# A two-layer decoder trunk in FP32: the offset term of two blocks of the last layer norm made on TensorE

## The chip, the cores and the metric

The kernel runs on one core of a Trainium2 chip. A core has five engines with queues of their own: PE (TensorE: matrix products into PSUM, with the weight loads shown apart as PEld), DVE (VectorE), ACT (ScalarE), POOL (GpSimd) and SP (SyncE, which here issues DMAs). The metric is the time of one execution on the device in microseconds (us), as a median of several runs.

## The reference, cut to what matters

Two layers over 256 positions of width 2048. The first has a gated short convolution, the second latent attention; each is followed by an MLP of width 8192 with squared ReLU, and each sub-layer ends in a layer norm of the scaled input plus the sub-layer's output. What matters here is the very last line, the layer norm behind the second MLP.

```python
def layer_norm(x, g, b):
    mu = jnp.mean(x, axis=-1, keepdims=True)
    var = jnp.mean(jnp.square(x - mu), axis=-1, keepdims=True)
    return (x - mu) * lax.rsqrt(var + LN_EPS) * g + b
...
for layer in range(2):
    mix = short_conv_mixer(...) if layer == 0 else mla_mixer(...)
    h = layer_norm(ALPHA * h + mix, ln_g[layer, 0], ln_b[layer, 0])
    h = layer_norm(ALPHA * h + sq_relu_mlp(h, ...), ln_g[layer, 1], ln_b[layer, 1])
return h
```

## The kernel before, in words

All products are made from FP32 values split into a high and a low part in a reduced format (`hi`, `lo`, type fp32r), with two or three TensorE products for each. Weights come from memory in pieces of 128 x 1024 into a pool of six buffers (`raws`, tag "raw"); ACT writes the high part, DVE subtracts it and writes the low part, into a ring of eight (`whl`). Activations stay in SBUF for the whole run. PSUM has eight banks of 128 x 512, in two pools of four, and `psum(name)` (line 228) takes one.

The order on each engine is made by a scheduler at build time. It goes through the instructions in the order in which the program wrote them, as a priority, and puts an instruction earlier where its engine would have nothing else that is ready. Only where `state["kept"]` is a set does the wrapper `Engine` (lines 60 to 79) pin it: the first instruction of each engine after that point is left free, and each further one goes behind the one written before it on its engine. So it is in the long middle of an MLP, whose order a planner (`Work`, lines 582 to 715) writes out. Everything around the change below is left to the scheduler.

**The start.** Lines 347 to 354 set a 128 x 128 tile `ones` (and two columns of `col`) and run ten TensorE products of `ones` with itself into a bank that nobody reads, while the first input is on its way (lines 527 to 542: sixteen rows of input and weights, converted by ACT and DVE as they land, then multiplied).

**The means' column.** `Norm.means` (line 387) makes one small column, `off`, in a buffer of its own, once, at the end of the first MLP's planned part.

**The end.** `to_out` (line 1331) takes over when the planned part of the second MLP is done. The result is held as 4 column blocks of 512 (n = 0 to 3) for 2 groups of 128 positions (t = 0, 1), each `block(n, t)` of 128 x 512 in SBUF. `turn_residual` adds the transposed input. The norm's gain and offset, `gbt`, spread over all 128 partitions, are loaded: `gbt[:, n, :BW]` is g of block n, `gbt[:, n, BW:]` is b. Then `down` (line 306) makes the last part of the products `ps_d` for blocks 0 and 1, both t together, and `down_late` (line 318) for blocks 2 and 3: first both blocks of t = 0, then both of t = 1. After each product `put` adds it into the block (DVE), and `counted` takes the block's statistics (DVE). When block 3 of a t is done, `finished` (line 1341) joins the statistics to mean and variance (`mv`), makes r = 1/sqrt(var + eps) in `rsqrt` (line 361: one ACT square root and four small DVE operations, `iv`, `rt`, `ra`, `rr`), and for each of the four blocks does two DVE operations and one DMA to the output:

```python
u = (d - mean) * g          # scalar_tensor_tensor, 128 x 512
d = u * r + b               # scalar_tensor_tensor, 128 x 512
sync.dma_start(out[...], d)
```

(The first two lines are lines 1354 and 1355 in short form.) The output of t = 0 is made while TensorE still works on t = 1; that of t = 1 comes after all products.

Of the kernel before, what the change touches and what calls it, by code (L numbers as in the profile page):

```python
# [10 lines left out]
F32 = mybir.dt.float32  # L11
F32R = mybir.dt.float32r
AF = mybir.ActivationFunctionType
ALU = mybir.AluOpType
AX = mybir.AxisListType

P = 128
# [16 lines left out]
NB = 4  # L34
BW = D // NB
# [18 lines left out]
def trunk(ctx: ExitStack, tc: tile.TileContext, opening, xT, vecs, w_in, w_out, w_kv, w_q, w_uk, w_uv,  # L54
          w_qn, w_qp, w_o, w1, w2, w2f, cosT, sinT, mask, ident, gb, out):
    nc = tc.nc
    PS = bass.MemoryType.PSUM
    state = {"made": 0, "next": 2 * OPEN, "kept": None}
# [22 lines left out]
    scalar, vector, tensor, sync = (Engine(e) for e in (nc.scalar, nc.vector, nc.tensor, nc.sync))  # L81
    const = ctx.enter_context(tc.tile_pool(name="const", bufs=1))
    act = ctx.enter_context(tc.tile_pool(name="act", bufs=1))
    raws = ctx.enter_context(tc.tile_pool(name="raws", bufs=RAW))
    whl = ctx.enter_context(tc.tile_pool(name="whl", bufs=WA))
    tmp = ctx.enter_context(tc.tile_pool(name="tmp", bufs=2))
    small = ctx.enter_context(tc.tile_pool(name="small", bufs=2))
# [5 lines left out]
    def array(tag, dtype, name, *dims):  # L93

        n = int(np.prod(dims))
        t = act.tile([P, ROOM[tag] // 4], dtype, tag=tag, name=name)[:, :n]
        names = "uvwxyz"[:len(dims)]
        return t.rearrange(f"p ({' '.join(names)}) -> p {' '.join(names)}", **dict(zip(names, dims)))
# [38 lines left out]
    start = [0]  # L137
# [3 lines left out]
    class Banks:  # L141
# [15 lines left out]
        @classmethod  # L157
        def next(cls):
            cls.count += 1
            if cls.only is not None:  # L160
                return cls.only
            return cls.more if cls.more is not None and cls.count % 8 >= 4 else pmm
# [65 lines left out]
    def psum(name):  # L228
        return Banks.next().tile([P, 512], F32, tag="mm", name=name)
# [76 lines left out]
    def down(x, put, n):  # L306

        ps = [psum("ps_d") for _ in range(2)]
        for j in range(len(x) // 2):
            w, = take(1)  # L310
            for kk in range(2):
                k = 2 * j + kk
                for t in range(2):
                    dot(ps[t], wide_rows(w, kk), held(x[k], t), k == 0, k == len(x) - 1)
        for t in range(2):
            put(n, t, ps[t])

    def down_late(x, put, blocks):

        ws = {}  # L320
        for t in range(2):
            for n in blocks:
                ps = psum("ps_d")
                for k in range(len(x)):
                    if (n, k // 2) not in ws:
                        ws[n, k // 2], = take(1)
                    dot(ps, wide_rows(ws[n, k // 2], k % 2), held(x[k], t), k == 0, k == len(x) - 1)
                put(n, t, ps)
# [17 lines left out]
    id_t = const.tile([P, P], F32, name="id_t")  # L346
    ones = const.tile([P, P], F32, name="ones")
    col = const.tile([P, COL], F32, name="col")
    vector.memset(ones, 1.0 / P)
    warm = psum("warm")  # L350
    for _ in range(WARM):
        tensor.matmul(warm[:, :P], ones, ones, start=True, stop=True)
# [5 lines left out]
        sync.dma_start(cos_t, cosT)  # L358
        sync.dma_start(sin_t, sinT)

    def rsqrt(out, ve):

        n = ve.shape[-1]
        s, iv, t, a = (small.tile([P, 2], F32, tag=g, name=g)[:, :n] for g in ("sq", "iv", "rt", "ra"))
        scalar.activation(s, ve, AF.Sqrt)
        vector.reciprocal(iv, ve)
        vector.tensor_tensor(t, s, iv, ALU.mult)
        vector.scalar_tensor_tensor(a, s, -0.5, t, ALU.mult, ALU.mult)
        vector.scalar_tensor_tensor(out, a, 1.5, t, ALU.add, ALU.mult)
# [6 lines left out]
    class Norm:  # L376
# [10 lines left out]
        def means(self):  # L387

            ps = psum("mu0c")
            for t in range(2):  # L390
                tensor.matmul(ps[:, t:t + 1], xres[:, 0, t * P:(t + 1) * P], ones[:, 0:1], start=True, stop=True)
            self.off = small.tile([P, 2], F32, tag="off", name="off", bufs=1)
            vector.tensor_scalar(self.off, ps[:, 0:2], -self.scale, None, ALU.mult)

        def prepare(self, m):
# [41 lines left out]
        def stats(self):  # L437

            st = psum("stat")
            for j in range(2):  # L440
                for b in range(2):
                    c = st[:, 2 * j + b:2 * j + b + 1]
                    tok = slice(b * P, (b + 1) * P)
                    tensor.matmul(c, (self.S, self.Q)[j][:, tok], col[:, 0:1], start=True, stop=True)
            nm = small.tile([P, 2], F32, tag="nm", name="nm")
            vector.tensor_scalar(nm, st[:, 0:2], -1.0, None, ALU.mult)
            ve = small.tile([P, 2], F32, tag="ve", name="ve")
            vector.tensor_tensor(ve, nm, nm, ALU.mult)
            vector.scalar_tensor_tensor(ve, st[:, 2:4], LN_EPS, ve, ALU.add, ALU.subtract)
            r = small.tile([P, 2], F32, tag="rr", name="rr")  # L450
            rsqrt(r, ve)
            return nm, r
# [97 lines left out]
    for m in range(NC):  # L550
# [3 lines left out]
        for what in "cub":  # L554
            ps = next(pss)
# [558 lines left out]
    with tc.tile_pool(name="att", bufs=1) as ap:  # L1114
# [35 lines left out]
        def rms(out, sqs):  # L1150

            st = psum("rstat")
            for b in range(2):
                tensor.matmul(st[:, b:b + 1], sqs[:, b * P:(b + 1) * P], col[:, 1:2], start=True, stop=True)
            ve = small.tile([P, 2], F32, tag="ve", name="rve")
            vector.tensor_scalar(ve, st[:, 0:2], RMS_EPS, None, ALU.add)
            rsqrt(out, ve)
# [24 lines left out]
        for m in range(NK):  # L1182
            ps = next(pss)
# [139 lines left out]
    def turn_residual(block):  # L1323
        for n in range(NB):
            for t in range(2):
                ps = psum("turned")
                for j in range(4):
                    tensor.transpose(ps[:, j * P:(j + 1) * P], xres[:, 4 * n + j, t * P:(t + 1) * P], id_t)
                vector.scalar_tensor_tensor(block(n, t), ps, ALPHA, block(n, t), ALU.mult, ALU.add)

    def to_out(block, put, h):
        turn_residual(block)
        gbt = array("b", F32, "gbt", NB, 2 * BW)
        for n in range(NB):
            sync.dma_start(gbt[:, n, :], gb[n].partition_broadcast(P))
        stats = small.tile([P, 2, NB, 10], F32, tag="stats", name="stats", bufs=1)[:, :, :, :6]

        def counted(n, t):
            vector.bn_stats(out=stats[:, t, n, :], in_=block(n, t))

        def finished(n, t, ps):
            put(n, t, ps)
            counted(n, t)
            if n < NB - 1:
                return
            mv = small.tile([P, 2], F32, tag="nm", name="mv")
            vector.bn_aggr(out=mv, in_=stats[:, t, :, :])
            ve = small.tile([P, 2], F32, tag="ve", name="ve")[:, :1]
            vector.tensor_scalar(ve, mv[:, 1:2], LN_EPS, None, ALU.add)
            r = small.tile([P, 2], F32, tag="rr", name="rr")[:, :1]  # L1350
            rsqrt(r, ve)
            for i in range(NB):
                d, u = block(i, t), raws.tile([P, 1024], F32, tag="raw", name="u")[:, :BW]
                vector.scalar_tensor_tensor(u, d, mv[:, 0:1], gbt[:, i, :BW], ALU.subtract, ALU.mult)
                vector.scalar_tensor_tensor(d, u, r, gbt[:, i, BW:], ALU.mult, ALU.add)
                sync.dma_start(out[t * P:(t + 1) * P, i * BW:(i + 1) * BW], d)

        for n in range(2):
            down(h, put, n)
            for t in range(2):  # L1360
                counted(n, t)
        down_late(h, finished, range(2, NB))

    with tc.tile_pool(name="fast2", bufs=1) as fast:
        mlp(3, after, None, to_out, fast)
# [88 lines left out]
```

## Time and profile before

| what | value |
|---|---|
| median of 3 runs | 1997.64 us (1997.62 to 1998.24) |
| the profiled execution | 1998.73 us |
| its span, first to last instruction | 1996.9 us |
| PE busy | 1983.1 us (99% of the span) |
| DVE busy | 1752.6 us (88%) |
| ACT busy | 1388.6 us (70%) |
| POOL busy | 2.3 us |
| mean granted TensorE clock | 0.998 of full |

The profile page is read from part 4, the chain of work that ended last, which says whose work filled the span, to the timelines, which list single instructions with start, duration, engine, operation and the tiles written and read. Nearly all instructions carry line 71, the line of the wrapper, so groups are told apart by tile names. A duration in a timeline holds an instruction's latency too: independent instructions of one engine overlap a little, so the step from start to start is what one costs in a row.

### The profile page before, as it was taken

What the parts mean: (1) busy time and instruction counts of PE and PEld (TensorE: products, weight loads), DVE (VectorE), ACT (ScalarE), POOL (GpSimd) and SP (SyncE); (2) the same over time, 40 slices, a digit from 0 to 9 for tenths busy, and PEclk for the clock granted to TensorE, in tenths of its full rate; (3) what the DMA queues carried; (4) which work ended last, traced back from release to release, by engine and by line L of the source; (5) the groups of instructions that cost most, each with busy time, mean ns of one, the idle gap of its engine ahead of it and who ended that gap; (6) DMA issues with size and microseconds to landing.
All of it is one profiled execution on the core that took longest, in us unless ns stands there. A gap on an engine that the chain in (4) does not pass through costs nothing.

```text
span 1996.9 us, 29770 instructions
## 1 busy us (share of the span) xinstructions
PE 1983.1 (99%) x11058; PEld 1735.0 (87%) x11058; DVE 1752.6 (88%) x2630; ACT 1388.6 (70%) x2069; POOL 2.3 (0%) x21
## 2 busy tenths in 40 slices
PE   9999999999999999999999999999999999999997
PEld 8888888988888888888889998898888888888886
DVE  7667667689999999999988888878999999999997
ACT  6444445577887888878856655567788788887871
POOL 0000000000000000000000000000000000000000
PEclk9999999999999999999999999999999999999999
DMA  9755556456666666666765543644666666666673
GB/s 341 230 188 189 191 186 188 156 164 195 208 200 202 205 202 205 200 202 207 221 208 158 165 129 117 204 163 154 201 203 206 200 203 204 202 206 202 199 248 110
DMA packets 107858, 387.39 MB, mean 194 GB/s; under 512 B 11969, under 2 KB 12737, under 8 KB 107713
## 3 DMA queue, kind: packets, MB, share of 16 engines
q1 hardware_dynamic: 107568, 385.36, 61.5%
q8 instruction: 86, 1.41, 0.3%
q14 instruction: 60, 0.48, 0.1%
q10 hardware_dynamic: 144, 0.13, 0.0%
HBM read 383.35 MB, written 2.10 MB: 193 GB/s over the span
## 4 chain that ended last, share of the span: by engine, by line
PE 98%; DVE 1%; issue 0%; ACT 0%; DVEq 0%
PE ps_m L71 31%; PE sum L71 27%; PE ps_u L71 20%; PE ps_d L71 4%; PE ps_w L71 4%; PE ps_g L71 4%; PE ps_q L71 1%; PE ps_v L71 1%; PE S L71 1%; PE ps_k L71 1%; PE ps_wo L71 1%; PE po L71 1%; PE ps_p L71 1%; PE turned L71 0%; DVE lo L71 0%
## 5 line engine op out<-in xcount | busy, mean ns | idle before, releaser
L71 DVE TENSOR_TENSOR lo<-w,hi 128x1024 fp32r<-128x1024 f32 x536 | 640.8, 1220 | 38.5 <-ACT hi L71 37.7
L71 ACT CAST hi<-w 128x1024 fp32r<-128x1024 f32 x536 | 541.8, 1061 | 64.2 <-DVE w L71 63.3
L71 ACT CAST hi<-raw 128x1024 fp32r<-128x1024 f32 x278 | 289.9, 1051 | 252.9 <-PE ps_u L71 155.0
L71 DVE TENSOR_TENSOR lo<-raw,hi 128x1024 fp32r<-128x1024 f32 x278 | 333.8, 1221 | 112.3 <-ACT hi L71 39.7
L71 PE MATMUL ps_m<-xhl,hi 128*128 128x512 f32 x1792 | 425.6, 390 | 0.0
L71 PEld LDWEIGHTS ps_m<-xhl,hi 128*128 128x128 f32 x1792 | 336.1, 188 | 71.7
L71 PE MATMUL sum<-hi,hc 128*128 128x512 f32 x736 | 278.0, 391 | 0.0
L71 PE MATMUL sum<-lo,hc 128*128 128x512 f32 x656 | 257.3, 392 | 0.0
L71 PE MATMUL sum<-hi,ha 128*128 128x512 f32 x640 | 246.5, 389 | 0.0
L71 PEld LDWEIGHTS ps_m<-xhl,lo 128*128 128x128 f32 x1792 | 229.8, 191 | 8.7
L71 PE MATMUL ps_m<-xhl,lo 128*128 128x256 f32 x1792 | 232.5, 283 | 0.0
L71 DVE TENSOR_TENSOR w<-w,w 128x512 f32<-128x512 f32 x312 | 213.7, 685 | 0.3
L71 PE MATMUL ps_u<-xhl_a,hi 128*128 128x512 f32 x704 | 168.1, 391 | 0.0
L71 PEld LDWEIGHTS sum<-hi,hc 128*128 128x128 f32 x736 | 138.6, 188 | 26.7 <-DVE t L71 0.3
L71 PEld LDWEIGHTS ps_u<-xhl_a,hi 128*128 128x128 f32 x704 | 129.4, 188 | 25.1
L71 PEld LDWEIGHTS sum<-hi,ha 128*128 128x128 f32 x640 | 120.2, 188 | 26.2
L71 PEld LDWEIGHTS sum<-lo,hc 128*128 128x128 f32 x656 | 123.6, 188 | 22.3
L71 ACT COPY sums<-sum 128x512 f32<-128x512 f32 x194 | 112.8, 596 | 12.3 <-PE sum L71 11.8
L71 ACT COPY t<-ps_m 128x256 f32<-128x256 f32 x112 | 42.4, 378 | 97.9 <-PE ps_m L71 97.9
L71 ACT COPY sum<-sums 128x512 f32<-128x512 f32 x174 | 105.4, 606 | 0.8
L71 PE MATMUL ps_w<-xd,hi 128*128 128x258 f32 x512 | 94.4, 284 | 0.5 <-DVE xres L71 0.5
L71 PEld LDWEIGHTS ps_u<-xhl_a,lo 128*128 128x128 f32 x704 | 90.3, 191 | 3.4
(201 smaller groups left out, 2785.4 us busy)
## 6 DMA issues: line engine op xcount, KB each, us to landing
w<-in_w_dram SPq DMA_DIRECT2D x224, 512.0 KB, 3.8
w<-in_w2f_dram SPq DMA_DIRECT2D x208, 512.0 KB, 4.3
raw<-in_w_in_dram SPq DMA_DIRECT2D x88, 512.0 KB, 4.5
raw<-in_w_dram SPq DMA_DIRECT2D x64, 512.0 KB, 4.4
raw<-in_w_out_dram SPq DMA_DIRECT2D x32, 512.0 KB, 4.2
raw<-in_w_o_dram SPq DMA_DIRECT2D x32, 512.0 KB, 3.7
raw<-in_w2f_dram SPq DMA_DIRECT2D x16, 512.0 KB, 4.6
row<-in_opening_dram SPq DMA_DIRECT2D x15, 384.0 KB, 5.0
```

The costliest lines, as they stand in the source:

```text
L71: ins = op(*args, **named)
```

## The change

1. `ones` is set by GpSimd and not by VectorE.
2. The column `off` takes its buffer from the tag "nm", which has two buffers and which `nm` and `mv` use as well; the tag "off" is gone.
3. In the last norm, for t = 1 only, blocks 0 and 1 are done in another form. Since (d - mean) * g * r + b = (d * g) * r + (b - mean * r * g), VectorE makes d * g (`dg`) as soon as block 2 of t = 1 is done, ahead of the statistics of block 3, into two of the "raw" buffers. TensorE makes the bracket in two PSUM banks (`offset`): first the identity times b, then, once r is known, a diagonal matrix of -mean * r times g on top. VectorE makes the factor -mean * r (`nmr`), ScalarE the diagonal matrix (`diag`, the identity scaled by that column). The last step for these blocks is d = dg * r + offset.
4. For blocks 2 and 3 of t = 1 the form is the old one. `u` of block 2 is written between the square root and the reciprocal, `u` of block 3 behind `nmr`, and the four last steps follow in the order of blocks 2, 3, 0, 1.
5. From the joining of the statistics of t = 1 on, all of this is pinned (`state["kept"]` is a set), with the first instruction of each engine free. For t = 0 the operations are the same as before; in the program's text all four `u` now come ahead of the four `d`.

```diff
-    vector.memset(ones, 1.0 / P)
+    nc.gpsimd.memset(ones, 1.0 / P)
...
-    def rsqrt(out, ve):
+    def rsqrt(out, ve, between=iter(())):
...
         scalar.activation(s, ve, AF.Sqrt)
+        next(between, None)
         vector.reciprocal(iv, ve)
...
-            self.off = small.tile([P, 2], F32, tag="off", name="off", bufs=1)
+            self.off = small.tile([P, 2], F32, tag="nm", name="off")
...
+        offs = {}
...
+        def room(name):
+            return raws.tile([P, 1024], F32, tag="raw", name=name)[:, :BW]
...
             counted(n, t)
             if n < NB - 1:
+                if t:
+                    for i in range(2):
+                        offs[i] = psum("offset"), room("dg")
+                        vector.tensor_tensor(offs[i][1], block(i, t), gbt[:, i, :BW], ALU.mult)
                 return
+            if offs:
+                state["kept"] = set()
+            for i in offs:
+                tensor.matmul(offs[i][0], id_t, gbt[:, i, BW:], start=True, stop=False)
             mv = small.tile([P, 2], F32, tag="nm", name="mv")
             vector.bn_aggr(out=mv, in_=stats[:, t, :, :])
             ve = small.tile([P, 2], F32, tag="ve", name="ve")[:, :1]
             vector.tensor_scalar(ve, mv[:, 1:2], LN_EPS, None, ALU.add)
             r = small.tile([P, 2], F32, tag="rr", name="rr")[:, :1]
-            rsqrt(r, ve)
-            for i in range(NB):
-                d, u = block(i, t), raws.tile([P, 1024], F32, tag="raw", name="u")[:, :BW]
-                vector.scalar_tensor_tensor(u, d, mv[:, 0:1], gbt[:, i, :BW], ALU.subtract, ALU.mult)
-                vector.scalar_tensor_tensor(d, u, r, gbt[:, i, BW:], ALU.mult, ALU.add)
+            rest = [i for i in range(NB) if i not in offs]
+            terms = {i: (u, ps) for i, (ps, u) in offs.items()}
+
+            def centred():
+                for i in rest:
+                    u = room("u")
+                    vector.scalar_tensor_tensor(u, block(i, t), mv[:, 0:1], gbt[:, i, :BW], ALU.subtract, ALU.mult)
+                    terms[i] = u, gbt[:, i, BW:]
+                    yield
+
+            steps = centred()
+            rsqrt(r, ve, steps if offs else iter(()))
+            if offs:
+                nr = small.tile([P, 2], F32, tag="nr", name="nmr")[:, :1]
+                vector.scalar_tensor_tensor(nr, mv[:, 0:1], -1.0, r, ALU.mult, ALU.mult)
+                diag = room("diag")[:, :P]
+                scalar.activation(diag, id_t, AF.Copy, scale=nr)
+                for i in offs:
+                    tensor.matmul(offs[i][0], diag, gbt[:, i, :BW], start=False, stop=True)
+            for _ in steps:
+                pass
+            for i in rest + list(offs):
+                d, (u, term) = block(i, t), terms[i]
+                vector.scalar_tensor_tensor(d, u, r, term, ALU.mult, ALU.add)
                 sync.dma_start(out[t * P:(t + 1) * P, i * BW:(i + 1) * BW], d)
+            state["kept"] = None
```

## The prediction

> **What bounds the kernel now.** I read the page first, its span, busy shares and chain, then the waits of PE, to see whether anything in the middle can still move.
>
> ```profile
> span 1996.9 us, 29770 instructions
> PE 98%; DVE 1%; issue 0%; ACT 0%; DVEq 0%
> PE warm L71 <- DVE col L71: 1.1, 1, 1.1
> PE rstat L71 <- DVE csq L71: 0.8, 1, 0.8
> PE ps_w L71 <- DVE xres L71: 0.5, 1, 0.5
> PE S L71 <- DVE kqva L71: 0.4, 1, 0.4
> PE lnAB L71 <- DVE rr L71: 0.2, 1, 0.2
> ```
>
> The chain is TensorE's for 98% of the span, and between its first product and its last TensorE waits 0.8 + 0.5 + 0.4 + 0.2 = 1.9 us in all. So the middle can give back 1.9 us at the very most; a change that leaves the number of products there alone acts only at the two ends. The chain's end says how long the second end is.
>
> ```profile
> 1942.51 43.56 PE ps_d L71 x192
> 1986.09 0.70 DVE sums L71
> ```
>
> The last stage of products runs without a hole: 192 products from 1942.51 to 1986.07, 0.227 us each. Then only DVE is on the path, to 1996.9: 10.8 us, 0.5% of the time. That tail, instruction by instruction (DVE's timeline, and the last two DMA issues on SP):
>
> ```profile
> 1986.09 0.69 DVE L71 TENSOR_TENSOR sums<-sums,ps_d 128x512 f32<-128x512 f32 x1 [1.96 <-PE ps_d L71]
> 1986.81 0.69 DVE L71 BATCH_NORM_STATS2 stats<-sums 128x6 f32<-128x512 f32 x1
> 1987.54 0.26 DVE L71 BATCH_NORM_AGGREGATE mv<-stats 128x2 f32<-128x24 f32 x1
> 1987.84 0.15 DVE L71 TENSOR_SCALAR ve<-mv 128x1 f32<-128x1 f32 x1
> 1987.91 0.74 DVE L71 SCALAR_TENSOR_TENSOR u<-sums,mv,gbt 128x512 f32<-128x512 f32 x1
> 1988.57 0.16 DVE L71 RECIPROCAL iv<-ve 128x1 f32<-128x1 f32 x1
> ...
> 1990.94 2.74 DVE L71 SCALAR_TENSOR_TENSOR sums<-u,rr,gbt 128x512 f32<-128x512 f32 x4
> ```
>
> ```profile
> 1993.05 0.33 SPq L71 DMA_DIRECT2D out_dram<-sums  x1
> 1993.71 0.33 SPq L71 DMA_DIRECT2D out_dram<-sums  x1
> ```
>
> The scheduler has already put the four `u` between the small operations of the square root, so `u` costs the tail not 4 x 0.74 but what it keeps DVE busy: 0.66 from `u` to `iv`. The four last steps end at 1990.94 + 2.74 = 1993.68, the last output DMA is issued 0.03 later, and 3.2 us of transfer and closing follow, which the change leaves as they are. So the time follows the end of the last `d`.
>
> **The change, part by part.**
>
> *DVE's tail.* For t = 1 two of four `u` leave it, and one small operation (`nmr`) comes in. With fewer `u` to fill the gaps, the small ones now wait for each other. What such a wait costs is in an earlier norm, where four of them run in a row, with a long one behind:
>
> ```profile
> 1330.03 0.15 DVE L71 TENSOR_TENSOR rt<-sq,iv 128x2 f32<-128x2 f32 x1
> 1330.21 0.16 DVE L71 SCALAR_TENSOR_TENSOR ra<-sq,rt 128x2 f32<-128x2 f32 x1
> 1330.41 0.16 DVE L71 SCALAR_TENSOR_TENSOR rr<-ra,rt 128x2 f32<-128x2 f32 x1
> 1330.61 0.16 DVE L71 TENSOR_TENSOR nr<-nm,rr 128x2 f32<-128x2 f32 x1
> 1330.69 1.23 DVE L71 TENSOR_TENSOR lo<-raw,hi 128x1024 fp32r<-128x1024 f32 x1
> ```
>
> That is 0.20 us a step when each needs the one before, 0.08 to one that doesn't. The pinned order gives: `u` of block 2 at 1987.91 as before, `iv` 1988.57, `rt` 1988.77, `ra` 1988.97, `rr` 1989.17, `nmr` 1989.37, `u` of block 3 at 1989.45, then `d` of block 2 at 1990.11, of block 3 at 1990.77, of block 0 at 1991.43. The two last `d` read their term from PSUM; the nearest row is this, against the form with all in SBUF:
>
> ```profile
> L71 DVE SCALAR_TENSOR_TENSOR sums<-u,rr,gbt 128x512 f32<-128x512 f32 x8 | 5.5, 747 | 0.1
> L71 DVE SCALAR_TENSOR_TENSOR sums<-turned,sums 128x512 f32<-128x512 f32 x8 | 5.0, 681 | 0.0
> ```
>
> So a `d` from PSUM takes 0.07 less, and its step is 0.60 where the other's is 0.66 (bounds: 0.60 to 0.66). `d` of block 1 starts at 1992.03 and ends at 1992.71: **0.97 us before** 1993.68, if the offsets are there.
>
> *Are they there?* The square root on ACT doesn't delay `rt`: it starts 0.04 after `ve` and takes 0.20.
>
> ```profile
> 1988.03 0.20 ACT L71 ACTIVATE sq<-ve 128x1 f32<-128x1 f32 x1 [10.68 <-DVE ve L71]
> L71 ACT ACTIVATE xd<-xres,vec 128x256 fp32r<-128x256 f32 x48 | 23.8, 496 | 0.0
> L71 PE MATMUL mu0p<-xres,ones x4: 377/380/483, 156.8 to 1212.7; 128*128 128x256 f32 x4
> 1985.66 0.39 PE L71 MATMUL ps_d<-hi,ha 128*128 128x512 f32 x1
> ```
>
> `diag`, 128 columns with a column as scale, lies between the 0.20 for 1 column and the 0.50 for 256: I take 0.40. `nmr` ends at 1989.53, so `diag` runs from 1989.57 to 1989.97. A product of plain FP32 operands is not in the trace with 512 columns. The one with 256 (`mu0p`) shows two passes a product (four records for two products) of 0.38 each; the reduced format streams 512 columns in 0.227 and shows 0.39, so 0.16 of a record is latency, and a plain pass of 256 columns streams in 0.22. With 512 I estimate 0.43 a pass and 0.86 a product (bounds 0.40 and 0.45 a pass). Adding 0.05 for the signal and 0.12 ahead of the first pass, `offset` of block 0 is written by 1990.14 + 0.86 + 0.16 = 1991.16, needed at 1991.43; that of block 1 by 1992.02, needed at 1992.03. With `diag` at 0.50 block 1 is late by 0.1. So the term from TensorE is just in time, and I cost it at nothing to 0.2.
>
> The two products of the identity with b come ahead of these: 1.72 us of TensorE. If they stand behind the last `ps_d` (starts at 1985.66, streams to 1985.89) they end at 1987.6, while DVE is at the statistics: hidden. SP's eight output DMAs stay eight, in another order of blocks for t = 1.
>
> *`dg`.* Two DVE products, 0.60 each (as the step with one tile more, above).
>
> ```profile
> 1966.23 1.21 DVE L71 TENSOR_TENSOR lo<-raw,hi 128x1024 fp32r<-128x1024 f32 x1
> 1983.44 0.69 DVE L71 BATCH_NORM_STATS2 stats<-sums 128x6 f32<-128x512 f32 x1
> L71 DVE TENSOR_TENSOR sums<-sums,ps_d 128x512 f32<-128x512 f32 x8 | 5.3, 683 | 8.3 <-PE ps_d L71 8.3
> ```
>
> DVE idles 1.96 ahead of the last `put` (first row of the tail), and 8.3 us behind `ps_d` over the stage. The statistics of block 2 end at 1984.13, both `dg` by 1985.4, the last `put` starts at 1986.09: hidden with 0.7 to spare; without that cover it would be 1.2. The buffers: the last weights leave the six "raw" ones at 1967.4 (first row); two `dg` and four `u` of t = 0 fill them, and the `u` of t = 0 are free before t = 1 needs three.
>
> *The start.*
>
> ```profile
> 0.73 0.13 POOL L561 MEMSET cbuf<- 128x2 f32 x2 [0.29 <-POOLq L1441]
> 0.83 0.17 DVE L71 MEMSET ones<- 128x128 f32 x1 [0.83 <-PEq L1441]
> 1.05 4.34 PEld L71 LDWEIGHTS warm<-ones 128*128 128x128 f32 x20 [1.05 <-DVE col L71]
> 5.34 2.00 PE L71 MATMUL ps_g<-xhl_a,hifirst 128*128 128x512 f32 x4
> L1118 POOL MEMSET kpe<- x1: 527/527/527, 999.4 to 999.4; 128x512 f32 x1
> ```
>
> POOL starts at 0.73. From 0.13 at most for 2 columns and 0.53 for 512, 128 columns take some 0.2: `ones` at 0.94, where DVE had it at 1.00. The warm-up, and the products queued behind it, start 0.06 earlier at best (bounds: 0.1 earlier, 0.3 later if POOL took as long as for 512). I take 0.05 of gain.
>
> *`off`* is one small column with two buffers to choose from, used once in the first MLP, and the other user's tile is long done: nothing.
>
> **Sum:** 0.97 + 0.05 = 1.0 us. Against the profiled execution's own 1998.73 (span 1996.9 and 1.8 around it) that is 1997.7. It lay 1.1 above the median of the runs, 1997.64, so I forecast **1996.6 us**, 0.05% faster: within the 0.2% (4 us) that is about what a measurement of this kernel can tell from no change.
>
> **The rivals.** *The clock halves under the diagonal products (slower).* TensorE's granted clock at the end, in three stretches:
>
> ```profile
> 1983.00:1986.90 3.90, 3.05 (x14) 2.20 (x12) 1.87 (x4) 0.00 (x0) 0.00 (x0) 1.00 0.38 141
> 1986.90:1990.30 3.40, 0.00 (x0) 0.00 (x0) 3.33 (x10) 0.20 (x1) 0.00 (x0) 1.00 0.00 0
> 1990.30:1996.90 6.60, 0.00 (x0) 0.00 (x0) 3.35 (x6) 0.00 (x0) 0.00 (x0) 0.50 0.43 159
> ```
>
> It is whole until 1990.30 and half after, 4.2 us behind the last product. Now TensorE rests from 1987.6 to 1990.1, 2.5 us, and then has work at the very moment at which the clock fell. If it still falls there, each of the four passes takes 0.86: `offset` of block 1 is written at 1990.14 + 3.44 + 0.16 = 1993.74, its `d` ends near 1994.5, and the tail is 0.8 longer than before: 1997.64 + 0.8 - 0.05 = 1998.4. Against it: the fall came after more idleness than there now is. [...]
>
> *The products with b stand too early (slower).* The first of them is not pinned and needs only the identity, `gbt` and a free bank; the second hangs on the first alone. If the scheduler sees TensorE idle anywhere in the 43.56 us of `ps_d`, it puts them there, and the chip has no such hole: 1.72 us more ahead of the last `put`, less 1.0: 1997.64 + 0.7 = 1998.4, and up to 1.6 above the time before if the longer rest then also halves the clock. For it: the rule of the scheduler. Against: `ps_d` stands earlier in the program, and the trace shows it always ready.
>
> *It doesn't shorten the tail.* `diag` or the products come later than estimated by some 1.0, DVE waits as long as it saved: 1997.6.
>
> *The order elsewhere moves.* The warm-up's start could change what the scheduler does in stages that aren't pinned. The gain is bounded by the 1.9 above; a loss is not bounded, but needs TensorE to wait where it doesn't now: 1996 to 2003.
>
> **How the numbers follow.** Forecast 0.55 (1996.1 to 1997.1 by the bounds and the spread of the runs); clock 0.12; early products 0.15; nothing gained 0.08; order elsewhere 0.10. To hold 8 in 10 the range takes in both rivals at 1998.4 and the spread of 0.6 among the runs: 1995.9 to 1998.9. Faster than 1993.6 would take 1.0 from the tail and more than the middle has: 0.01. Slower than 2001.6 comes only from the order elsewhere: 0.03. Within 0.2%: 0.96.
>
> **What would show it.** Right: in the tail of the new profile `rt`, `ra`, `rr`, `nmr` 0.20 apart, the last `d` ending 5.9 us behind the last statistics' start (before: 6.9), the products with b behind the last `ps_d`, the clock at 1.00 through the diagonal ones. Wrong: DVE idle ahead of the last two `d`, released by PE; products named `offset` among the `ps_d`; PE waits in the middle above 1.9; a first `ps_g` later than 5.34.

## The result and the profile after

The kernel after takes 1993.74 us (median of 12 runs, 1992.49 to 1994.41) against 1998.15 (12 runs, 1997.62 to 1998.62) of the kernel before: ratio 0.9978, with a 95% interval of 0.9970 to 0.9985. It is 4.4 us faster. The forecast was 1.0 us, and the range ended at 1995.9. One of the eight executions of the run called e6 below took 5112.14 us at a whole clock; nothing on record says why, and the range given there leaves it out. The profiled execution of after took 1993.89 us, with this span and these shares of the chain that ended last.

```profile
span 1992.1 us, 29789 instructions
...
PE 98%; DVE 1%; ACT 0%; issue 0%; POOL 0%; ACTq 0%; DVEq 0%; POOLq 0%
```

First, where along the span did the two executions part? The chain of waits of the kernel after has the last products and what follows them at these places (start, length).

```profile
1937.80 43.58 PE ps_d L71 x192
...
1981.40 0.70 DVE sums L71
```

The last stage of products starts at 1937.80, where it was 1942.51. So 4.7 us were gained **before** the part that the change is about. From the last `put` (1981.40; before 1986.09) to the end of the span it is 10.7 us, before 10.8. The tail gave almost nothing. PE's waits (total, times, longest) do not explain the gain either.

```profile
PE offset L71 <- ACT diag L71: 2.3, 1, 2.3
PE warm L71 <- POOL cbuf L562: 1.0, 1, 1.0
PE rstat L71 <- DVE csq L71: 0.8, 1, 0.8
PE ps_w L71 <- DVE xres L71: 0.5, 1, 0.5
PE S L71 <- DVE kqva L71: 0.4, 1, 0.4
```

The three middle ones are as they were. What changed is how closely the products follow each other in the two MLPs. Two stretches of both kernels, with busy time and number of instructions in brackets, PE first: before,

```profile
447.00:976.00 529.00, 529.00 (x2705) 451.91 (x2704) 510.54 (x660) 436.32 (x615) 0.00 (x0) 1.00 0.67 203
1390.00:1922.00 532.00, 532.00 (x2718) 454.38 (x2717) 513.52 (x664) 437.96 (x617) 0.00 (x0) 1.00 0.66 204
```

and after:

```profile
447.00:976.00 529.00, 528.99 (x2713) 453.54 (x2712) 512.49 (x661) 437.89 (x617) 0.00 (x0) 1.00 0.66 205
1390.00:1922.00 532.00, 531.99 (x2730) 456.17 (x2729) 516.22 (x667) 439.29 (x619) 0.00 (x0) 1.00 0.67 205
```

PE is busy without a hole in all four, at a clock of 1.00, yet after does 8 and 12 products more in the same time. At the 0.196 us that a product of these stretches takes on the mean (529.00 / 2705) that is 20 x 0.196 = 3.9 us, in the two stretches alone. A busy share of 100% hid it. Among the groups of PE one stands out: the products that stream the tile `t` (the `t4` of the fast scheme, 128 x 1024, formed once in each of 104 rounds). Its rows give least, median and longest duration in ns, then the first and the last start. Before:

```profile
L71 PE MATMUL sum<-t,hc x216: 393/397/399, 447.8 to 1921.0; 128*128 128x512 f32 x108
L71 PE MATMUL sum<-t,ha x96: 397/397/398, 489.8 to 1921.2; 128*128 128x512 f32 x96
```

After:

```profile
L71 PE MATMUL sum<-t,hc x216: 389/389/389, 447.5 to 1916.3; 128*128 128x512 f32 x108
L71 PE MATMUL sum<-t,ha x96: 388/389/389, 489.2 to 1916.6; 128*128 128x512 f32 x96
```

The last start is 4.7 us earlier, the first only 0.3. The loss isn't confined to these three products of a round. PE's timeline of one round, before,

```profile
458.17 0.86 PE L71 MATMUL sum<-t,hc 128*128 128x512 f32 x3
458.87 0.39 PE L71 MATMUL sum<-hi,ha 128*128 128x512 f32 x1
...
459.56 3.80 PE L71 MATMUL ps_m<-xhl,hi 128*128 128x512 f32 x16
```

and after:

```profile
457.81 0.84 PE L71 MATMUL sum<-t,hc 128*128 128x512 f32 x3
458.49 0.39 PE L71 MATMUL sum<-hi,ha 128*128 128x512 f32 x1
...
459.17 3.79 PE L71 MATMUL ps_m<-xhl,hi 128*128 128x512 f32 x16
```

Three products with `t` and three behind them take 1.39 us before and 1.36 after. Over all 104 rounds, from the first product with `t` to the twelfth start behind it is 2767.0 ns before in the mean and 2726.5 after: 0.0405 us x 104 = 4.2 us.

Why would `t` stream differently? Its code isn't touched. But one line of the change frees a buffer: without the tag "off", 32 bytes wide, all that stands behind it in SBUF moves down by 32 bytes. In the built kernels `t` begins at byte 224,928 of each partition before and at 224,896 after. All other tiles that TensorE streams or loads in the MLPs (`hi`, `lo`, `xhl`, `ha`, `hc`) stand in both at the same remainder of 256 bytes, 128; `t` is at 160 before and at 128 after.

The tail, in DVE's timeline of the kernel after:

```profile
1981.40 0.69 DVE L71 TENSOR_TENSOR sums<-sums,ps_d 128x512 f32<-128x512 f32 x1 [1.01 <-PE ps_d L71]
...
1983.88 0.15 DVE L71 RECIPROCAL iv<-ve 128x1 f32<-128x1 f32 x1
1984.14 0.16 DVE L71 TENSOR_TENSOR rt<-sq,iv 128x1 f32<-128x1 f32 x1
1984.33 0.16 DVE L71 SCALAR_TENSOR_TENSOR ra<-sq,rt 128x1 f32<-128x1 f32 x1
1984.52 0.16 DVE L71 SCALAR_TENSOR_TENSOR rr<-ra,rt 128x1 f32<-128x1 f32 x1
1984.72 0.16 DVE L71 SCALAR_TENSOR_TENSOR nmr<-mv,rr 128x1 f32<-128x1 f32 x1
...
1985.45 1.41 DVE L71 SCALAR_TENSOR_TENSOR sums<-u,rr,gbt 128x512 f32<-128x512 f32 x2
1986.78 0.74 DVE L71 SCALAR_TENSOR_TENSOR sums<-dg,rr,offset 128x512 f32<-128x512 f32 x1
1988.17 0.75 DVE L71 SCALAR_TENSOR_TENSOR sums<-dg,rr,offset 128x512 f32<-128x512 f32 x1 [0.65 <-PE offset L71]
```

From the last `put` to the end of the last `d` it is 7.52 us; before, 7.59. The chain of small steps is as planned, but the last `d` waits for `offset`. PE's timeline and the granted clock (third number from the end) around it:

```profile
1981.20 1.88 PE L71 MATMUL offset<-gbt,id_t 128*128 128x512 f32 x4
1985.42 2.71 PE L71 MATMUL offset<-gbt,diag 128*128 128x512 f32 x4 [2.35 <-ACT diag L71]
```

```profile
1983.20:1985.40 2.20, 0.00 (x0) 0.00 (x0) 1.99 (x8) 0.60 (x2) 0.00 (x0) 1.00 0.00 0
1985.40:1986.60 1.20, 1.18 (x3) 0.68 (x4) 1.20 (x3) 0.00 (x0) 0.00 (x0) 0.98 0.00 0
1986.60:1988.20 1.60, 1.53 (x2) 0.00 (x0) 0.95 (x3) 0.00 (x0) 0.00 (x0) 0.50 0.73 270
```

After a rest of 2.35 us the diagonal products start at the whole clock, and 1.1 us later it halves under them. The mean clock of the span points to the runs that have this, since the earlier the clock falls the lower it is: it is 0.998 or 0.999 in nine of the twelve (1993.70 to 1994.41 us) and 1.000 in three (1992.49, 1992.72, 1992.81).

### The profile page after: what moved, and what is told of

Its sections match the earlier page's. It is cut to its first block, busy times and chain, and to the rows that moved or that the text cites. A ratio compares the mean times of both kernels' runs of the same rounds, so it can differ in the third digit from the quotient of the medians.

```text
span 1992.1 us, 29789 instructions
## 1 busy us (share of the span) xinstructions
PE 1983.0 (100%) x11066; PEld 1736.1 (87%) x11066; DVE 1752.1 (88%) x2630; ACT 1388.6 (70%) x2070; POOL 2.4 (0%) x22
## 4 chain that ended last, share of the span: by engine, by line
PE 98%; DVE 1%; ACT 0%; issue 0%; POOL 0%; ACTq 0%; DVEq 0%; POOLq 0%
PE ps_m L71 31%; PE sum L71 27%; PE ps_u L71 20%; PE ps_d L71 4%; PE ps_w L71 4%; PE ps_g L71 4%; PE ps_q L71 1%; PE ps_v L71 1%; PE S L71 1%; PE ps_k L71 1%; PE ps_wo L71 1%; PE po L71 1%; PE ps_p L71 1%; PE turned L71 0%; PE tp L71 0%; DVE lo L71 0%
## 5 line engine op out<-in xcount | busy, mean ns | idle before, releaser
L71 ACT ACTIVATE sf<-sf 128x512 f32<-128x512 f32 x120 | 76.5, 638 | 27.9 <-DVE sf L71 27.8
```

What stands on the lines that cost most here:

```text
L71: ins = op(*args, **named)
```

## The experiments

The theory: the gain is `off` alone, through the place of `t`, and the last norm gains nothing because the clock halves. The rivals: the last norm or the start does it by another order; another tile that moved does it; the place counts by itself, or only against the other operands.

**`off` alone, `off` in two buffers, and the rest without `off`.** The first and the second are the kernel before with one line changed, the third is the kernel after with that line as it was.

```diff
# e1_off_alone
-            self.off = small.tile([P, 2], F32, tag="off", name="off", bufs=1)
+            self.off = small.tile([P, 2], F32, tag="nm", name="off")
# e2_off_two_buffers
-            self.off = small.tile([P, 2], F32, tag="off", name="off", bufs=1)
+            self.off = small.tile([P, 2], F32, tag="off", name="off", bufs=2)
# e3_after_off_back
-            self.off = small.tile([P, 2], F32, tag="nm", name="off")
+            self.off = small.tile([P, 2], F32, tag="off", name="off", bufs=1)
```

> The kernel before, with one edit alone: the means' column takes its buffer from the tag nm. Layout theory: with its own buffer of 32 bytes gone, everything that lies behind it in SBUF moves down by 32 bytes, so the tile t of the MLPs starts at a multiple of 64 bytes, and the products that stream it no longer lose time: 4.4 us less than before (1993.7 where before has 1998.1), with the spacing of the products sum<-t at 227 ns instead of 234. Rival, the end and the start do it: this kernel has neither, so it is the same as before within 0.3 us.

> The kernel before, with the means' column in a tag of its own as there, but with two buffers for it instead of one (only one is ever used): everything behind moves up by 32 bytes, which also brings the tile t to a multiple of 64. Layout theory: 4.4 us less than before, as with the column in nm. Rival, sharing the tag nm is what helps (another order or a wait that goes): nothing is shared here, so 0.

> The kernel after, with the means' column back in a buffer of its own, so that t lies at 32 past a multiple of 64 again. Layout theory: the 4.4 us are lost, what is left is the start (0.1 to 0.3) and the new end (0.1 where the clock halves, 1.2 where it doesn't): 0.2 to 1.0 us less than before, 1997.1 to 1997.9. Rival, the last norm and the start bring the 4.4: it stays at 1993.7.

Measured: `off` alone 1993.56 (1993.37 to 1994.09), ratio 0.9978 [0.9970, 0.9987]; two buffers 2000.68, ratio 1.0013 [1.0004, 1.0022]; the rest without `off` 1996.82, ratio 0.9997 [0.9988, 1.0006]. One line that stores two columns elsewhere has the whole gain. In e1 the products with `t` have the duration that they have in after:

```profile
L71 PE MATMUL sum<-t,hc x216: 389/389/389, 446.7 to 1915.7; 128*128 128x512 f32 x108
```

e2 moves `t` the other way, 32 bytes further up (64 from its place in after), and is 2.6 us slower than before, where 4.4 us less were expected. So a place 64 bytes away isn't a good one, and an explanation by who shares the buffer falls: `off` shares it with nobody here, as in before, and the time isn't that of before.

e3 shows the last norm's part with an earlier fall of the clock, 0.3 us into the diagonal products. In its profiled execution the last `put` is at 1985.60, and the last `d` reads as follows:

```profile
1993.16 0.75 DVE L71 SCALAR_TENSOR_TENSOR sums<-dg,rr,offset 128x512 f32<-128x512 f32 x1 [0.96 <-PE offset L71]
```

The tail is 1993.91 - 1985.60 = 8.3 us there, 0.7 longer than before. Seven of its eleven runs have a clock of 1.000 and lie at 1996.56 to 1996.88, the other four at 1998.46 to 1998.88: one group below the expected 1997.1 to 1997.9, one above it.

**Only `t` moved.** The kernel after, with `t` 32 bytes further and all else in its place; and the kernel before, with `t` at a multiple of 256 bytes, which is 128 bytes from its place in after.

```diff
# e4_t_at_32, in after
-                    box["f"] = fast.tile([P, 2, BW], F32R, tag="t4", name="t4", bufs=1)
+                    box["f"] = fast.tile([P, 2 * BW + 8], F32R, tag="t4", name="t4", bufs=1)[:, 8:].rearrange("p (a c) -> p a c", a=2)
# e5_t_at_128, in before
-                    box["f"] = fast.tile([P, 2, BW], F32R, tag="t4", name="t4", bufs=1)
+                    box["f"] = fast.tile([P, 2 * BW + 24], F32R, tag="t4", name="t4", bufs=1)[:, 24:].rearrange("p (a c) -> p a c", a=2)
```

> The kernel after, with the tile t made 32 bytes larger and used from its byte 32 on: t lies at 32 past a multiple of 64, all other tiles where they are in the kernel after (the two tiles sf at multiples of 64). If it is t, read by TensorE: 4.4 us more than the kernel after, 0.2 to 1.0 below before, with the spacing of sum<-t back at 234 ns. If it is sf, which ACT and DVE write and read: as the kernel after, 1993.7.

> The kernel before, with one edit alone: the tile t is made 96 bytes larger and used from its byte 96 on, so that it starts at a multiple of 128 bytes; nothing else moves (sf stays at 32 past a multiple of 64, the means' column in its own buffer). With t at 32, 64 and 0 past a multiple of 128 the three kernels before, the one with two buffers and the one with the column in nm differ as 0, +2.6 and -4.5 us. Theory, t alone and its place within 128 bytes: 4.4 us less than before, 1993.7, with sum<-t at 227 ns. Rival, it is the place of sf or of the tiles of the attention that moved along: 0. Rival, the places count within 256 or more (t is here at 0 past a multiple of 256, all other streamed tiles at 128): a spacing that is neither 227 nor 234.

Measured: e4 1998.39 (1996.59 to 1998.73), ratio 0.9999 [0.9990, 1.0007]: the gain is gone, and it was `t`, not the other tile that moved (`sf`). The median lies 0.3 us above before, not 0.2 to 1.0 below as expected, and the mean clock parts these runs as well: those with 1.000 take 1996.59 to 1997.44, the others 1998.39 to 1998.73, in the median 4.0 and 4.9 us above their like in after. e5 1997.32, ratio 0.9997 [0.9988, 1.0006]: a miss. A well aligned `t` is nearly as slow as a badly aligned one; the row of e5 still differs from after's.

```profile
L71 PE MATMUL sum<-t,hc x216: 387/395/398, 447.7 to 1920.1; 128*128 128x512 f32 x108
```

So the form of the theory in which alignment by itself is the cause falls, and what is left is the place of `t` against the other operands, which in before and after all start at a remainder of 128 bytes.

**No rest for TensorE, and `ones` by DVE again.** Both are the kernel after; e6 adds ten products of `ones` with itself into a bank that nobody reads.

```diff
# e6_no_rest, behind the products of the identity with b
+            if offs:
+                idle = psum("idle")
+                for _ in range(WARM):
+                    tensor.matmul(idle[:, :P], ones, ones, start=True, stop=True)
# e7_ones_dve
-    nc.gpsimd.memset(ones, 1.0 / P)
+    vector.memset(ones, 1.0 / P)
```

> The kernel after, with ten small products of ones with itself, into a bank that nobody reads, behind the products of the identity with b, so that TensorE has work until the diagonal matrix is there. Theory, the clock halves under the diagonal products because TensorE rests before them: these products then take 0.43 a pass and not 0.85, the last step waits for nothing, and all runs lie at 1992.6, where the kernel after has three of twelve (mean clock 1.000) and the other nine at 1993.8: 1.1 us below its median. Rival, the products are slow for another reason (plain FP32 of 512 columns, or the bank read while they write): no change, 1993.7, or 0.1 more.

> The kernel after, with ones set by VectorE again. The trace of after has the warm-up 0.06 us earlier than before: so 0.06 us more than the kernel after, not to be told from it in time (1993.7 to 1993.9), with the warm-up's start back at 1.05. Rival, the earlier start decides when the clock rises: 0.2 to 1 us more.

Measured: e6 1992.79 (1992.32 to 1993.09), ratio 0.9974 [0.9963, 0.9984], with a clock of 1.000 in every run. It is the fastest of all versions. PE's timeline, DVE's last steps and the clock in e6:

```profile
1981.93 2.39 PE L71 MATMUL idle<-ones 128*128 128x128 f32 x20
1984.45 1.98 PE L71 MATMUL offset<-gbt,diag 128*128 128x512 f32 x4
```

```profile
1980.42 0.69 DVE L71 TENSOR_TENSOR sums<-sums,ps_d 128x512 f32<-128x512 f32 x1 [1.01 <-PE ps_d L71]
...
1984.48 1.41 DVE L71 SCALAR_TENSOR_TENSOR sums<-u,rr,gbt 128x512 f32<-128x512 f32 x2
1985.81 1.41 DVE L71 SCALAR_TENSOR_TENSOR sums<-dg,rr,offset 128x512 f32<-128x512 f32 x2
```

```profile
1985.40:1986.60 1.20, 1.03 (x3) 0.19 (x1) 1.20 (x3) 0.00 (x0) 0.00 (x0) 1.00 0.43 159
```

Nothing waits now: the tail is 1987.22 - 1980.42 = 6.80 us, 0.79 shorter than before and 0.72 shorter than in after. The ten products cost no time on the path: the diagonal ones start 0.05 us behind the end of `diag`, as in after. e7 took 1994.11 (1992.45 to 1994.18), 0.9979 [0.9970, 0.9988]: who sets `ones` can't be told from the time.

**Thirteen places of `t` in one run, and everything moved together.** In e9 each round begins `t` at another place; in e10 all tiles that TensorE uses in the MLPs stand 32 bytes further, `t` among them.

```diff
# e9_thirteen_places, in after
+PLACES = [b // 4 for b in (0, 16, 32, 48, 64, 96, 128, 160, 192, 224, 256, 288, 320)]
...
-                    box["f"] = fast.tile([P, 2, BW], F32R, tag="t4", name="t4", bufs=1)
+                    box["f"] = fast.tile([P, 2 * BW + 80], F32R, tag="t4", name="t4", bufs=1)[:, PLACES[i % 13]:][:, :2 * BW].rearrange("p (a c) -> p a c", a=2)
# e10_all_at_32, in after, behind the constants' pool
+    pads = ctx.enter_context(tc.tile_pool(name="pad", bufs=1))
...
+    nc.gpsimd.memset(pads.tile([P, 8], F32, name="pad"), 0.0)
```

> The kernel after, with t begun at thirteen places by turns: 0, 16, 32, 48, 64, 96, 128, 160, 192, 224, 256, 288 and 320 bytes beyond its place in after, group by group. Nothing else moves. Theory R (what counts is where t lies against the other operands of TensorE, and it repeats every 256 bytes): the rounds at 0 and at 256 keep 226.7 ns a product throughout; those at 32 and 288 lose some 42 ns a round as in before, those at 64 and 320 some 65, those at 128 some 36; the time is 1993.7 + 104 x 11/13 x 0.042 = 1997.4. Rival R' (the place in after is the only good one, or it repeats in a longer step): 256 loses as much as 128, 288 and 320 need not be like 32 and 64, the time is 1997.8. Rival A (multiples of a size, wherever the others lie): 0, 64, 128, 192, 256 and 320 are all alike and fast; 64 and 128 alone have spoken against it so far. Open is what 16 and 48 do, and whether some place is better than 0: then a round there has products closer than 226.7 ns.

> The kernel after, with 32 bytes put ahead of all the tiles that TensorE streams or loads in the MLPs (inputs, weights' high and low parts, products' inputs, t), so that all of them stand 32 bytes further and keep their places among themselves; only the constants' tiles stay. Theory R (the place of one operand against the other counts): as after, 1993.7 (1992.5 to 1994.4), 226.7 ns in every MLP round. Rival A (each operand has to lie at a multiple of 128 by itself): at least what moving the weights alone cost, 2018, with t's 4.4 on top 2022.

Measured: e10 1993.55 (1992.27 to 1994.02), ratio 0.9975 [0.9966, 0.9985]: as after, though `t` stands at the very byte (224,928) where before had it. **The absolute place didn't count here; the place against the other operands did.**

e9 took 1996.18 (1995.97 to 1997.84), 1.2 less than I had worked out from the median of after; six of its ten executions, and only three of the twelve of after, have a mean clock of 1.000. Its trace gives each place eight rounds. From the first product with `t` to the twelfth start behind it, medians in ns:

| bytes beyond the place in after | 0 | 16 | 32 | 48 | 64 | 96 | 128 | 160 | 192 | 224 | 256 | 288 | 320 |
|---|---|---|---|---|---|---|---|---|---|---|---|---|---|
| twelve products, ns | 2720 | 2776 | 2767 | 2780 | 2789 | 2753 | 2760 | 2747 | 2760 | 2747 | 2720 | 2767 | 2789 |

All eight rounds of a place agree within 1 ns, but for two rounds at 256 in which one product starts some 0.05 us late. The columns for 256, 288 and 320 repeat those for 0, 32 and 64: the step is 256 bytes, and of the ten remainders tried only that of the other operands is free of loss. The values at 32, 64 and 128 are also the medians of before and e4 (2767), of e2 (2789) and of e5 (2760): the single edits and the table are one effect. Two rounds in PE's timeline of e9, at 64 and at 0 bytes:

```profile
529.86 0.63 PE L72 MATMUL sum<-t,hc 128*128 128x512 f32 x2
...
531.26 2.01 PE L72 MATMUL ps_m<-xhl,hi 128*128 128x512 f32 x8
```

```profile
540.26 0.62 PE L72 MATMUL sum<-t,hc 128*128 128x512 f32 x2
...
541.62 2.20 PE L72 MATMUL ps_m<-xhl,hi 128*128 128x512 f32 x9
```

Six products take 1.40 us at the one place and 1.36 at the other.

**Only the weights' ring moved.** If what is streamed counts against what is loaded, moving the ring (`hi`, `lo`: loaded in `ps_m`, streamed in `sum`) must slow products in which `t` has no part. In e8 32 bytes stand ahead of the ring and 96 behind it, so that `t` moved too, to 128 beyond its place in after (the 64 in the expectation of e11 is wrong). In e11 and e12 the bytes ahead and behind make 256, and `t` keeps its remainder.

```diff
# e8_ring_at_32, in after; e11 has pads of 8 and 56 columns, e12 of 32 and 32
+    pads = [ctx.enter_context(tc.tile_pool(name="pad0", bufs=1))]
     whl = ctx.enter_context(tc.tile_pool(name="whl", bufs=WA))
+    pads.append(ctx.enter_context(tc.tile_pool(name="pad1", bufs=1)))
...
+    for i, pool in enumerate(pads):
+        nc.gpsimd.memset(pool.tile([P, (8, 24)[i]], F32, tag="pad", name=f"pad{i}"), 0.0)
```

> The kernel after, with a pad of 32 bytes ahead of the ring that holds hi and lo and one of 96 behind it: hi and lo lie at 32 past a multiple of 128, all else at the same place within 128 bytes as in the kernel after. Theory A, a streamed operand off a multiple of 128 is slow in itself: each of some 2500 products that stream 512 columns of hi or lo costs 7.4 ns more, as sum<-t at 32 on the mean: 18 us more, 2012, steady over the long rows of sum. Theory B, it is the change of place from one product to the next that costs: the long rows of sum stay at 227 ns, and only the first products behind a change of operand (to t, to xhl) lose 30 to 40 ns in all, four changes in each of 104 rounds: 8 to 15 us more. Rival, t is slow for something of its own (written by ACT and DVE just before): 0.

> The kernel after, with 32 bytes ahead of the ring of the weights' high and low parts and 224 behind it, so that the ring alone moves (by 32 bytes) and everything else keeps its place within 256 bytes, t too; in the run with the ring at 32 t had also stood 64 bytes further. Theory R (the place of what is streamed against what is loaded counts, step 256): nearly as that run, 2018.3 less the 312 products with t, which took 5 ns each too long there, 1.6 us: 2016.7 (2015 to 2018.5); ps_m<-xhl,hi at 396 ns a record as there, sum<-hi,hc at 394, sum<-t,hc back near 389. Rival (what moved besides the ring made the loss): at most 7 us above after, 2001, with ps_m<-xhl,hi at 389 to 391.

> The kernel after, with the ring alone moved by 128 bytes (128 ahead of it and 128 behind). Theory R with step 256: slow too, though the ring is at a multiple of 128; by the first three products with t at 128 (234, 224 and 238 ns, mean 232.0) against those at 32 (235.8, 230.8, 235.8, mean 234.1), 5.3 / 7.4 of the ring's 23 us: 2010 (2006 to 2016). Rival (a step of 128 for the ring): as after, 1993.7, with ps_m<-xhl,hi at 389 ns.

Measured: e8 2018.26, ratio 1.0103 [1.0087, 1.0118]; e11 2019.84, ratio 1.0110 [1.0092, 1.0128]; e12 2017.07, ratio 1.0095 [1.0077, 1.0113]. e8 lies above what either of its theories gave, and both fall: by A `ps_m`, which streams nothing of the ring, should not have been slower, and by B the long rows of `sum` should have stayed at 227 ns (`sum<-hi,ha`: 232.3). The groups of PE (busy us, mean ns) in after, e11 and e12, one fence each:

```profile
L71 PE MATMUL ps_m<-xhl,hi 128*128 128x512 f32 x1792 | 424.6, 389 | 0.0
L71 PE MATMUL sum<-hi,hc 128*128 128x512 f32 x736 | 277.9, 391 | 0.0
```

```profile
L71 PE MATMUL ps_m<-xhl,hi 128*128 128x512 f32 x1792 | 436.9, 396 | 0.0
L71 PE MATMUL sum<-hi,hc 128*128 128x512 f32 x736 | 280.4, 395 | 0.0
```

```profile
L71 PE MATMUL ps_m<-xhl,hi 128*128 128x512 f32 x1792 | 434.5, 394 | 0.0
L71 PE MATMUL sum<-hi,hc 128*128 128x512 f32 x736 | 279.9, 394 | 0.0
```

In `ps_m` the streamed `xhl` stands where it stood; only what is loaded as weights moved, by 32 or 128 bytes, and from start to start it is 233.8 and 232.4 ns instead of 226.8. So what counts there is the place of the streamed operand against the ring, from which TensorE loads, and 128 bytes apart is no better in kind than 32. It isn't so for every shape: the products of 256 columns, `ps_m<-xhl,lo`, stand closer inside their rows with the ring moved, 118.1 ns in e11 and 118.9 in e12 instead of 119.9. e11 and e12 both lie above the range that I gave. One detail was a miss: I expected the products with `t` back near 389 ns in e11, since `t` and `hc` had not moved; they stay at 394, and e11 is 1.6 us slower than e8, not 1.6 faster. That slow products all round them delay them is my reading: the rounds of before show products that don't read `t` spaced up to 236 ns behind those that do, but no run here tests it by itself. Why the loss differs from place to place (27 ns a round at 160, 69 at 64) isn't explained by any run here. Nor is it shown whether the accesses of ACT and DVE, which write `t` and the ring, have a part in it.

## Why the prediction was wrong, point by point

- **"So the middle can give back 1.9 us at the very most": this is the step that failed**, and with it "`off` ... nothing". Waits of PE bound what a change of order can give back, not what a product costs. I took 0.227 us for every product of 512 columns, from the last stage, though the records of 393 to 399 ns against 389 in the MLPs were there to see; and I looked at `off` as a buffer to wait for, not as 32 bytes ahead of other tiles. Worth, by e1 and the kernel before beside it: 1998.06 - 1993.56 = 4.5 us, that is, all of it. The same bound closed off the rival of an order that moves elsewhere, and none of the signs of being wrong that I listed would have shown a closer spacing of products.
- *DVE's tail* (0.97 us less). The mechanism was right, and with the clock whole (e6) it gives 0.79. `rt`, `ra`, `rr`, `nmr` are 0.19 to 0.20 apart as said. The mis-sized terms: `rt` starts 0.26 behind `iv` and not 0.20, and a `d` with its term in PSUM has a step of 0.66, not 0.60, and takes 0.74 to 0.75, not 0.68: 0.06 + 0.06 + 0.06 = 0.18. The row that I took as the nearest (`sums<-turned,sums`) doesn't stand for it; no run shows what makes the difference.
- *Are the offsets there?* `diag` takes 0.40 as estimated (1984.97 to 1985.37), and a pass (1.88 - 0.59) / 3 = 0.43 us, as estimated (0.59 is the record of one pass at the whole clock). The 0.05 for the signal and the 0.12 ahead of the first pass stood in no row that I showed; in after and e6 the first pass starts 0.05 behind the end of `diag`, and its record is 0.11 longer than the next (0.70 and 0.59), so both were nearly right. With a whole clock nobody waits for them (e6); with a halved one the last `d` waits 0.65.
- *The products with b* stand behind the last `ps_d`, and both `dg` are hidden: one at 1975.25 even ahead of the `d` of t = 0, and DVE still idles 1.01 us ahead of the last `put`. The rival of products that come too early is out.
- *The start:* 0.06 us earlier (0.99 against 1.05), POOL's `ones` in 0.20 us, both as said.
- *The rival with the clock*, to which I gave 0.12, is by their mean clock and time what happens in nine of twelve runs of after. Its size depends on the moment of the fall: in after's trace it came 1.1 us into the diagonal products, and the tail is 0.07 shorter than before; in e3's it came 0.3 us into them, and the tail is 0.7 longer, near the 0.8 that I had worked out. I argued that the earlier fall had come after more idleness; a rest of 2.35 us was enough. What I gave 0.08, that the tail isn't shorter, is the outcome in after's profile, by this cause.

The forecast was a gain of 1.0 at the ends and nothing between. The runs show 4.5 between, and at the ends some 0.8 with a whole clock and nearly nothing, or a loss, without.

## What to carry to other kernels

A change of a buffer can act through the addresses of tiles that it doesn't touch (here 32 bytes and 4.5 us): compare the built layouts before putting a time to such an edit, and compare the number of products in an equal stretch of time, since busy shares and waits showed nothing here. Here products of 512 columns were closest where the operand that TensorE streams and the one it loads start at the same remainder of 256 bytes; 32 bytes were worth 0.2% in a tile that three products of each round stream, and 1.3% in the ring of the weights (2019.84 against 1993.74). Where TensorE rested 2.35 us ahead of its last work, products that nobody reads kept its clock whole in every run of e6, at no cost on the path.

## What the runs showed of the hardware that was not expected

- The spacing of products of 512 columns depended on the places of their operands against each other, with a step of 256 bytes: 226.7 ns at the same remainder; in `ps_m`, with the ring moved, 232.4 (by 128 bytes) and 233.8 (by 32) in the mean. The prediction didn't reckon with the place; measured were 4.5 us for `t` (e1, 1993.56 against 1998.06) and some 26 for the ring (e11, 2019.84 against 1993.74). What makes the difference isn't shown.
- The clock fell after a rest of 2.35 us, but not every time. In after's trace it fell 1.1 us into the diagonal products, in e3's 0.3 us into them. In e4 the products come behind the same rest, and all four passes run at the whole clock, 1.98 us instead of the 2.71 in after (the row of e4):

```profile
1989.13 1.98 PE L71 MATMUL offset<-gbt,diag 128*128 128x512 f32 x4 [2.35 <-ACT diag L71]
```

  So the same rest cost 1.5 us in e3 (a tail of 8.3 us, against 6.80 in e6, where products fill it) and nothing in e4's passes. By mean clock and time the outcome differs from run to run of one kernel: three of the twelve runs of after have 1.000 and at most 1992.81 us, the other nine 0.998 or 0.999 and at least 1993.70. What decides between them isn't shown, and no run varied the rest's length.
- The start differed between two executions: in before the first four products took 2.00 us, and the trace's record of the whole clock begins at 7.15 us; in e1, with the start of before instruction for instruction, they took 1.16. Why isn't shown.

```profile
5.17 1.16 PE L71 MATMUL ps_g<-xhl_a,hifirst 128*128 128x512 f32 x4
```
